# Cross attention's output projection as seven block products, its weight sums made on GpSimd and kept in DRAM

## The chip, the cores and the metric

The kernel runs on one core of one Trainium2 chip. The metric is the device time of one execution in microseconds (us). A core has five engines with a queue each: TensorE (PE in the profile, its weight loads PEld), VectorE (DVE), ScalarE (ACT), GpSimd (POOL) and SyncE (SP), which issues the DMAs. Each engine runs its own instructions in their order, and waits on semaphores for the others.

## The reference

One layer of an encoder on 1024 tokens of width 1024 in fp32: a mixer (window attention beside a gated delta rule), cross attention of 4 heads into 256 memory tokens, and a SwiGLU FFN, each with an RMSNorm before and after and a residual. The change is in the second of these, at `@ w_co`, and in what follows it up to the FFN's first products.

```python
def _memory_cross_attention(h, mem_n, w_q, w_kv, w_o):
    q = (h @ w_q).reshape(b, s, CROSS_HEADS, CROSS_HEAD_DIM)
    ...
    p = jax.nn.softmax(jnp.einsum('bqhd,bkhd->bhqk', q, k) * (CROSS_HEAD_DIM ** -0.5), axis=-1)
    o = jnp.einsum('bhqk,bkhd->bqhd', p, v).reshape(b, s, D_MODEL)
    return o @ w_o
...
c = _memory_cross_attention(_rms_norm(x, g_cross_pre), _rms_norm(mem, g_mem), w_cq, w_ckv, w_co)
x = x + _rms_norm(c, g_cross_post)
f = _swiglu(_rms_norm(x, g_ffn_pre), w_gate_up, w_down)
x = x + _rms_norm(f, g_ffn_post)
```

## The kernel before

Every matrix that goes into a product is split into a high part, rounded to the matmul's format by a cast on ACT, and a low part, the difference, on DVE or on POOL (`split`, L102 and L103). A product takes three matmuls: high by high, high by low, low by high. Weights come in pieces of 512 KB by `load_w` (L127): a DMA from SP into one of two buffers `wraw`, the cast to `whi`, the subtraction to `wlo`. A scheduler puts the instructions of each engine in an order before the kernel runs; `load_w` has a raised priority, so that pieces are asked for early, and the two buffers bound how early.

The tokens go in two halves of 512, four tiles of 128 each. **Cross attention** runs over 8 steps (half, head): `cross_q` makes two of the eight columns of q from two pieces of `w_cq`, whose low parts are POOL's; `cross_attention` is a generator that makes scores (`pcs`), softmax (`cpr`), transposes (`pct`) and the head's output (`pco`), and `go_on` lets it advance beside the steps that follow. Each output is split out of PSUM (`po`) into the place of q, in `q0` or `q1`, where it is the operand of the next product.

**The output projection** is `mid_gemm` with `w_co`, once for each half of the tokens and in it once for each half of the 1024 columns: four pieces of the weight by four token tiles by two row blocks by three matmuls, 96 matmuls of 512 columns, 384 in all (L1021). The last steps of the attention run inside the first of them (`rest`). Each result is squared on ACT for the norm (L1024) and multiplied by the gain on DVE (L1025). After both column halves the residual `xr` is loaded (L1031), the norm's factor comes from POOL (L1033, L1034), DVE makes the residual sum (L1035), which is stored, ACT squares it (L1038), POOL makes the next factor (L163, L164), and DVE scales it into `xr` (L1044).

**The turn.** `turned_k` transposes the normed tokens (L1187). For the first half that happens while the second half's projection runs: ACT scales `xraw` (L1192), casts it, and POOL subtracts the low part. For the second half it happens beside the FFN's first products (`pA0`, `EARLY` = 4 steps, L1224), whose results are copied to `m1` (L1241); the FFN itself works on block sums of the two halves (T1 to T4), made in that turn.

Of the kernel before, what the change touches and what calls it, by code (L numbers as in the profile page):

```python
# [19 lines left out]
P = 128  # L20
# [26 lines left out]
def host_constants():  # L47
# [24 lines left out]
    return out  # L72


@with_exitstack
def tile_hybrid_block(
# [112 lines left out]
    d_x1 = dram.tile([S, D], F32, name="d_x1")  # L189
    d_x2 = dram.tile([S, D], F32, name="d_x2")  # L190
# [780 lines left out]
    opB_first = [opB.tile([P, KT, HALF], t, tag=n, name=n) for n, t in ((b0, F32R), (b1, F32), (b2, F32R))]  # L971
# [3 lines left out]
    places = {"s1": ((opB, b0), (opB3, "b3")), "s2": ((opB, b1), (opB, b2))}  # L975

    def operand(pool_, tag):
        if tag in places:
            return [p_.tile([P, KT, HALF], F32R, tag=t, name=t) for p_, t in places[tag]]
        return [pool_.tile([P, KT, HALF], F32R, tag=f"{tag}{i}", name=f"{tag}{i}") for i in range(2)]  # L980
# [20 lines left out]
    def mid_gemm(tz, act, w, gp, res, dst, hf, between=None, eng=None, then=None, second=None):  # L1001
# [24 lines left out]
        xn = []  # L1026
        for t in range(4):
            tok = slice(hf * HALF + t * P, hf * HALF + (t + 1) * P)
            z = zs[t]
            xr = tz.tile([P, D], F32, tag="xr", name="xr", bufs=XR)  # L1030
            nc.sync.dma_start(xr, res[tok, :])  # L1031
            rs = tz.tile([P, 1], F32, tag="prs", name="prs", bufs=4)
            nc.gpsimd.tensor_scalar(rs, sss[t][:, 1:2], sss[t][:, 0:1], D * EPS, ALU.add, ALU.add)  # L1033
            nc.gpsimd.tensor_tensor(rs, rs, mhalf[:, 0:1], ALU.pow)  # L1034
            nc.vector.scalar_tensor_tensor(z, z, rs, xr, ALU.mult, ALU.add)  # L1035
            nc.sync.dma_start(dst[tok, :], z)
            s2 = tz.tile([P, 1], F32, tag="ps2", name="ps2", bufs=4)
            nc.scalar.activation(xr, z, AF.Square, accum_out=s2)  # L1038
            r2 = tz.tile([P, 1], F32, tag="pr2", name="pr2", bufs=4)
            rstd_of(r2, s2, 1.0 / D, EPS)  # L1040
            if hf and not eng:
                nc.scalar.activation(xr, z, AF.Identity, scale=r2)
            else:
                nc.vector.tensor_scalar(xr, z, r2, None, ALU.mult)  # L1044
            xn.append(xr)
        return xn
# [26 lines left out]
    h2T = [[opB.tile([P, KT, HALF], F32R, tag=b1, name=b1), opB_first[2]]]  # L1073
# [23 lines left out]
    def cross_attention(q, h):  # L1097
# [65 lines left out]
    def blocks(t):  # L1163
        return t[:, 0:HK], t[:, HK:KT]

# [387 lines left out]
```

## Time and profile before

| what | value |
|---|---|
| median of 3 runs | 1539.52 us (1538.82 to 1541.98) |
| the profiled execution | 1539.27 us |
| its span, in which the profile's times lie | 1537.3 us |
| granted TensorE clock | 0.99 |

The span is the time between the first and the last instruction that the profiler saw; the execution's time has 1.97 us around it. A row of the timeline begins with the start in the span and the length, then engine, line, operation, what is written and read, and in brackets how long the engine was idle before it and what ended that. A row such as "TENSOR_TENSOR wlo<-wraw,whi 128x1024" is one instruction on 128 partitions by 1024 elements; "x2" joins two in a row, with the length of both.

### The profile page before, as it was taken

Reading aid. Unit: us, or ns where it says so; the run is one execution under the profiler, and the core shown is the slowest. Engines: PE = TensorE matmul, PEld = TensorE weight load, DVE = VectorE, ACT = ScalarE, POOL = GpSimd, SP = SyncE. Lnnn points to the kernel's source line nnn. Section 1 sums busy time; section 2 is a strip of 40 time slices with the busy share of each in tenths; the row PEclk is TensorE's granted clock in tenths of the full one; section 3 lists DMA queues with packets and bytes.
Section 4 is the critical chain, followed back from the end, with each engine's and each line's share of the span. In section 5 each row is a group of like instructions: output and inputs, shape, how many; then the busy total and the mean of one; then the engine's idle time right before and its main releaser. Section 6 shows DMA issues by size and latency. Waiting matters only on the chain.

```text
span 1537.3 us, 20939 instructions
## 1 busy us (share of the span) xinstructions
PE 1485.0 (97%) x7451; PEld 1251.2 (81%) x7451; DVE 1062.2 (69%) x1762; ACT 713.2 (46%) x1377; POOL 307.0 (20%) x297
## 2 busy tenths in 40 slices
PE   6999999988999989999999999999999999999998
PEld 5888887877899878888888887888888888888786
DVE  6877898856989766445444487776877555696665
ACT  5665551336556765455444564323223332354532
POOL 2000110000004201252201432443433332000010
PEclk8999999999999999999999999999999999999999
DMA  6235456768997575354113554343533334852355
GB/s 207 76 112 142 121 154 153 223 170 257 326 312 249 167 272 177 116 192 137 55 56 99 185 195 130 120 133 110 172 123 96 110 103 158 287 189 95 107 177 166
DMA packets 267366, 247.16 MB, mean 161 GB/s; under 512 B 39016, under 2 KB 204797, under 8 KB 267261
## 3 DMA queue, kind: packets, MB, share of 16 engines
q1 hardware_dynamic: 267261, 245.82, 51.1%
q8 instruction: 59, 0.97, 0.3%
q14 instruction: 46, 0.38, 0.1%
HBM read 173.65 MB, written 69.50 MB: 158 GB/s over the span
## 4 chain that ended last, share of the span: by engine, by line
PE 82%; DVE 7%; DMA 3%; ACT 3%; issue 2%; SPq 1%; POOL 0%; DVEq 0%; POOLq 0%; ACTq 0%
PE pg L263 12%; PE pmg L1021 10%; PE pD L1224 8%; PE pE L1224 8%; PE pA L1224 8%; PE pcq L263 6%; PE pdX L1414 6%; PE pdA L1414 4%; PE pB L1224 4%; PE psc L787 2%; PE pdX L1507 2%; PE pdD L1414 2%; PE pcs L1108 1%; PE pco L1136 1%; PE pcv L934 1%
## 5 line engine op out<-in xcount | busy, mean ns | idle before, releaser
L102 ACT CAST whi<-wraw 128x1024 fp32r<-128x1024 f32 x108 | 113.4, 1050 | 174.9 <-PE pmg L1021 55.2
L103 DVE TENSOR_TENSOR wlo<-wraw,whi 128x1024 fp32r<-128x1024 f32 x78 | 95.2, 1221 | 85.6 <-ACT whi L102 78.6
L263 PE MATMUL pg<-hhi,whi 128*128 128x512 f32 x352 | 141.1, 402 | 1.5 <-DVE rop L732 1.3
L263 PE MATMUL pg<-hlo,whi 128*128 128x512 f32 x352 | 140.7, 400 | 0.0
L263 PE MATMUL pg<-hhi,wlo 128*128 128x512 f32 x352 | 140.3, 399 | 0.0
L1021 PE MATMUL pmg<-whi,b 128*128 128x512 f32 x384 | 116.1, 391 | 0.0
L1224 PE MATMUL pA<-s,whi 128*128 128x512 f32 x352 | 109.2, 391 | 1.0 <-ACT m L1241 1.0
L103 POOL TENSOR_TENSOR wlo<-wraw,whi 128x1024 fp32r<-128x1024 f32 x30 | 72.6, 2420 | 160.7 <-ACT whi L102 160.6
L1021 PEld LDWEIGHTS pmg<-whi,b 128*128 128x128 f32 x384 | 71.7, 188 | 14.5
L263 PEld LDWEIGHTS pg<-hhi,whi 128*128 128x128 f32 x352 | 67.3, 192 | 15.6 <-DVE rop L732 1.8
L263 PEld LDWEIGHTS pg<-hlo,whi 128*128 128x128 f32 x352 | 67.5, 192 | 13.3
L263 PEld LDWEIGHTS pg<-hhi,wlo 128*128 128x128 f32 x352 | 67.3, 191 | 13.2
L1414 PE MATMUL pdX<-dhl,whi 128*128 128x512 f32 x264 | 76.1, 390 | 1.5 <-DVE zv L1469 0.8
L1224 PEld LDWEIGHTS pA<-s,whi 128*128 128x128 f32 x352 | 65.5, 188 | 14.7 <-ACT m L1241 1.5
L1021 PE MATMUL pmg<-wlo,b 128*128 128x512 f32 x192 | 71.2, 390 | 0.0
L1224 PE MATMUL pA<-s,wlo 128*128 128x512 f32 x176 | 68.7, 391 | 0.0
L102 ACT CAST whi<-araw 128x1024 fp32r<-128x1024 f32 (+1 forms) x36 | 35.4, 982 | 71.3 <-PE pdX L1414 27.6
L1301 POOL TENSOR_TENSOR act<-act,up 128x512 f32<-128x512 f32 x33 | 50.2, 1520 | 89.4 <-DVE up L1300 53.1
L103 DVE TENSOR_TENSOR wlo<-araw,whi 128x1024 fp32r<-128x1024 f32 (+1 forms) x36 | 40.8, 1134 | 39.1 <-ACT whi L102 39.0
L288 DVE SCALAR_TENSOR_TENSOR acc<-cp,cols,acc 128x1024 f32<-128x1024 f32 x48 | 61.3, 1280 | 1.5 <-ACT acc L286 0.8
L1414 PEld LDWEIGHTS pdX<-dhl,whi 128*128 128x128 f32 x264 | 49.3, 188 | 12.8 <-issue 1.1
L102 ACT CAST dhl<-b 128x512 fp32r<-128x512 f32 x66 | 40.2, 619 | 32.8 <-PE pdA L1414 18.5
(410 smaller groups left out, 3950.9 us busy)
## 6 DMA issues: line engine op xcount, KB each, us to landing
wraw<-in_w_gate_up_dram SPq DMA_DIRECT2D x52, 512.0 KB, 4.0
kv<-d_kv SPq DMA_DIRECT2D x32, 512.0 KB, 6.7
wraw<-in_w_in_dram SPq DMA_DIRECT2D x22, 512.0 KB, 5.0
b<-in_w_down_dram SPq DMA_DIRECT2D x20, 512.0 KB, 6.9
araw<-d_as SPq DMA_DIRECT2D x20, 512.0 KB, 3.8
pz<-d_pz SPq DMA_DIRECT2D x32, 256.0 KB, 6.3
wraw<-in_w_ckv_dram SPq DMA_DIRECT2D x16, 512.0 KB, 7.1
wraw<-in_w_out_dram SPq DMA_DIRECT2D x16, 512.0 KB, 3.9
```

The source lines that it names most:

```text
L102: nc.scalar.copy(hi, src)
L103: (eng or nc.vector).tensor_tensor(lo, src, f32(hi), ALU.subtract)
L263: nc.tensor.matmul(p_, w[:, k, :], ah[a][:, k, :], start=(k == 0 and i == 0), stop=(k == nk - 1 and i == 2))
L288: nc.vector.scalar_tensor_tensor(acc, cp[:, t:t + S], taps[t], acc, ALU.mult, ALU.add)
L787: nc.tensor.matmul(out[:, d, h, :], lt[:, d, h, :], rt[:, d, h, :], start=True, stop=True)
L934: nc.tensor.matmul(pp[t], mT[a][:, k, t * P:(t + 1) * P], w[:, kk, :], start=(k == 0 and i == 0), stop=(k == KT - 1 and i == 2))
L1021: nc.tensor.matmul(pp[t], act[a][:, k, tt], w_[:, kk, :], start=(k == 0 and i == 0), stop=(k == KT - 1 and i == 2))
L1108: nc.tensor.matmul(pp[:, t2_, :], q[a][:, ct, tt], kr_[b_][:, ct, :], start=(j == 0 and i == 0), stop=(j == 1 and i == 2))
L1224: nc.tensor.matmul(out_, w[a][:, k, :], xx[b_][:, k, :], start=(start and k == 0 and i == 0), stop=(k == HK - 1 and i == 2), skip_group_ch ...
L1301: nc.gpsimd.tensor_tensor(o_, o_, up, ALU.mult)
L1414: nc.tensor.matmul(banks[t], a[:, k - k0, tt], w, start=(first and k == 0 and i == 0), stop=(k == NB - 1 and i == 2), skip_group_check=not ...
L1507: nc.tensor.matmul(X[t], a[:, k], w[:, k0 + k], start=False, stop=(k0 + k == NB - 1 and i == 2), skip_group_check=True)
```

## The change

The product of all tokens with `w_co` is written as a 2 by 2 block product (token halves by row halves, row halves by column halves) in Winograd's form, with seven products of blocks in the place of eight. Rows are regrouped so that block row r takes the 256-row pieces 2kp + r, which are the columns that the even or the odd heads made.

- The attention's outputs are copied to fp32 (`araw` for the first half, `araw1` for the second) before they are split. For the first half, and for the odd heads of the second, POOL makes the low part from the copy; before, it was DVE, out of PSUM.
- `weight_sums`: in steps 0, 1, 3 and 4 of the attention four blocks of `w_co` are loaded into the buffers of z, POOL makes four sums of them in place, 128 x 1024 each, and POOL issues their stores to `d_t` in DRAM, from which `load_w` fetches them later.
- `token_sums`: DVE makes four sums of token blocks and splits S1 and S2, for the first pair of heads inside the first product and for the second pair after it.
- The products, in order: q0's even heads by w11, then its odd heads by w21 on top, S2, S1 on top, S4 by w22, S3, and q1's odd heads on top; each is 48 matmuls.
- The first half's turn (`turn_first`) stands between the two halves of the last product; the residual's second four loads wait for it, since `xr` has four buffers.
- The second half's turn begins after one early step of the FFN instead of ahead of it, and T1's and T3's low parts go from DVE to POOL.

```diff
+    def attended(q, hf, h, j, po):
...
+        nc.scalar.copy(raw, po)
+        if h % 2 or not hf:
+            split(q[0][:, ct, :], q[1][:, ct, :], raw, eng=nc.gpsimd)
...
-            split(q[0][:, 2 * h + j, :], q[1][:, 2 * h + j, :], po)
+            attended(q, hf, h, j, po)
...
+    def weight_sums(step, kp):
+        if step == 0:
+            for t, rc in zip(wt, ((0, 0), (0, 1), (1, 1), (1, 0))):
+                nc.sync.dma_start(t, co(*rc, kp).rearrange("(k p) n -> p k n", p=P))
+        elif step == 1:
+            for o_, a, b_, d_ in ((b11, b12, b11, d_t[0]), (b12, b22, b12, d_t[1]), (b22, b22, b11, d_t[2]), (b21, b21, b22, d_t[3])):
+                nc.gpsimd.tensor_tensor(o_, a, b_, ALU.subtract)
+                nc.gpsimd.dma_start(d_[kp * 256:(kp + 1) * 256, :].rearrange("(k p) n -> p k n", p=P), o_)
...
-        turns.append(cross_attention(q, h))
...
+        turns.append(cross_attention(q, hf, h))
+        if i < 6:
+            weight_sums(i % 3, i // 3)
...
+    def token_sums(p):
+        k2 = slice(2 * p, 2 * p + 2)
+        a11, a12, a21, a22 = araw[2 * p], araw[2 * p + 1], araw1[2 * p], araw1[2 * p + 1]
+        nc.vector.tensor_tensor(a22, a21, a22, ALU.add)
+        nc.vector.tensor_tensor(a21, a11, a21, ALU.subtract)
+        nc.vector.tensor_tensor(a11, a22, a11, ALU.subtract)
+        split(S2h[:, k2], S2l[:, k2], a11)
+        nc.vector.tensor_tensor(a12, a12, a11, ALU.subtract)
+        split(S1h[:, k2], S1l[:, k2], a22)
...
-    xn = mid_gemm(tz, q0, w_co, gp, d_x1, d_x2, 0, then=rest)
+        if i == 1:
+            token_sums(0)
+
+    def token_product(banks, a, w, start=True, halves=False, then=None, between=None):
...
+            for t in ts:
+                for kk in range(2):
+                    k = 2 * kp + kk
+                    for i, (b_, c) in enumerate(((0, 0), (0, 1), (1, 0))):
+                        nc.tensor.matmul(banks[t], a[c](k, slice(t * P, (t + 1) * P)), pieces[kp][b_][:, kk, :],
...
+    token_product(A, heads(q0, 0), lambda kp: co(0, 0, kp), then=rest)
+    for t in range(4):
+        nc.scalar.copy(zz[t][:, HI], A[t])
+    token_product(A, heads(q0, 1), lambda kp: co(1, 0, kp), start=False, then=lambda kp: rest(2 + kp))
...
+    token_sums(1)
+    for t in range(4):
+        square(0, t, 0, A[t], zz[t][:, LO])
+        nc.vector.tensor_tensor(zz[t][:, LO], A[t], gp[:, LO], ALU.mult)
...
+    token_product(X, tiles((S2h, S2l)), summed(2))
+    for t in range(4):
+        nc.vector.tensor_tensor(z1[:, t, LO], zz[t][:, HI], X[t], ALU.add)
...
+        split(S4h[:, k2], S4l[:, k2], araw[2 * p + 1])
+    token_product(X, tiles((S1h, S1l)), summed(0), start=False)
...
+        split(S3h[:, k2], S3l[:, k2], araw1[2 * p], eng=nc.gpsimd)
+    X = four([(pg, "pg")] * 4)
+    token_product(X, tiles((S4h, S4l)), lambda kp: co(1, 1, kp), halves=True)
...
+        xn.append(normed(tz, 0, t, zz[t], zss[0][t], d_x1, d_x2))
+    X = four(others)
+    token_product(X, tiles((S3h, S3l)), summed(1))
+    for t in range(4):
+        z = z1[:, t, HI]
+        nc.vector.tensor_tensor(z, z, X[t], ALU.add)
+        square(1, t, 1, z)
+        scaled(z, HI, nc.gpsimd)
...
+    def turn_first():
+        for k in range(KT):
+            pt = turned_k(xn, k, (pg, "pg"))
+            nc.scalar.activation(raw[:, k, :], pt, AF.Identity, scale=gain("ffn", k))
+            split(x1h[:, k, :], x1l[:, k, :], raw[:, k, :], eng=nc.gpsimd)
...
+    token_product(X, heads(q1, 1), summed(3), start=False, halves=True, between=turn_first)
+    xn = []
+    for t in range(4):
+        z = z1[:, t, LO]
+        nc.vector.tensor_tensor(z, z, X[t], ALU.add)
+        square(1, t, 0, z)
+        scaled(z, LO)
+        xn.append(normed(tz, 1, t, z1[:, t], zss[1][t], d_x1, d_x2))
...
+            split(T1[0][:, k], T1[1][:, k], t1, eng=nc.gpsimd)
+            split(T3[0][:, k], T3[1][:, k], t3_, eng=nc.gpsimd)
...
+        if e == 1:
+            T1, T2, T3, T4 = turn_second()
```

Three places of the engines' orders follow. Numbers behind the names are buffers; with the change `split` is at L117 and L118.

On DVE, where the attention ends: before, the last head's two outputs are split and the wlo of the following pieces come.

```order
L1025 TENSOR_TENSOR z_7880<-pmg_7888,gpost_7875 128x512
L103 TENSOR_TENSOR wlo_8169<-wraw_8166,whi_8168 128x1024
L1025 TENSOR_TENSOR z_7881<-pmg_7889,gpost_7875 128x512
L103 TENSOR_TENSOR b2_7295<-pco_8124,b1_7294 128x512
L103 TENSOR_TENSOR b2_7295<-pco_8133,b1_7294 128x512
L103 TENSOR_TENSOR wlo_8199<-wraw_8196,whi_8198 128x1024
```

With the change, at the end of the attention and of the first pair of products (araw_6855, araw_6856, araw1_8056 and araw1_8163 are the outputs of heads 2 and 3 of the two halves; s00 and s01 are the high and low parts of S1 and S2, b0_8297 and b3_8298 those of S3 and S4):

```order
L1224 TENSOR_TENSOR araw1_8163<-araw1_8056,araw1_8163 128x1024
L1288 TENSOR_TENSOR z_6851<-pmg_7951,gpost_6846 128x512
L1225 TENSOR_TENSOR araw1_8056<-araw_6855,araw1_8056 128x1024
L118 TENSOR_TENSOR wlo_8266<-wraw_8263,whi_8265 128x1024
L1288 TENSOR_TENSOR z_6852<-pmg_7952,gpost_6846 128x512
L1226 TENSOR_TENSOR araw_6855<-araw1_8163,araw_6855 128x1024
L118 TENSOR_TENSOR b3_8298<-araw_6854,b0_8297 128x1024
L118 TENSOR_TENSOR s01_7940<-araw1_8163,s00_7939 128x1024
L1228 TENSOR_TENSOR araw_6856<-araw_6856,araw_6855 128x1024
L118 TENSOR_TENSOR s01_7940<-araw_6855,s00_7939 128x1024
```

The second s01 row is the low part of S2 that the S2 product's second half reads; nine instructions stand ahead of it from the first sum of these heads on.

On POOL, in the attention before, there is only the low part of each piece of `w_cq`:

```order
L103 TENSOR_TENSOR wlo_7299<-wraw_7296,whi_7298 128x1024
L103 TENSOR_TENSOR wlo_7392<-wraw_7389,whi_7391 128x1024
L103 TENSOR_TENSOR wlo_7443<-wraw_7440,whi_7442 128x1024
L103 TENSOR_TENSOR wlo_7536<-wraw_7533,whi_7535 128x1024
L103 TENSOR_TENSOR wlo_7587<-wraw_7584,whi_7586 128x1024
```

With the change the sums, their stores and the low parts of the heads' outputs stand between them:

```order
L1193 TENSOR_TENSOR z_6849<-z_6850,z_6849 128x1024
L118 TENSOR_TENSOR wlo_7352<-wraw_7349,whi_7351 128x1024
L1194 DMA d_t1_121<-z_6849 128x2x512
L1193 TENSOR_TENSOR z_6850<-z_6851,z_6850 128x1024
L1194 DMA d_t3_122<-z_6850 128x2x512
L1193 TENSOR_TENSOR z_6851<-z_6851,z_6849 128x1024
L118 TENSOR_TENSOR wlo_7445<-wraw_7442,whi_7444 128x1024
L1194 DMA d_t2_123<-z_6851 128x2x512
```

Three to four sums and stores now stand between one wlo and the next.

On ACT, in the turn of the first half: before, the groups come in pairs, with casts of weights and squares of the projection between them.

```order
L1192 ACTIVATE xraw_8328<-ptn_8331,cols_73 128x512
L1192 ACTIVATE xraw_8328<-ptn_8339,cols_73 128x512
L102 CAST s00_8329<-xraw_8328 128x512 x2
L102 CAST whi_8541<-wraw_8539 128x1024
L1192 ACTIVATE xraw_8328<-ptn_8347,cols_73 128x512
```

With the change, the last part of it, with the squares of the second half (z1) and the copies that free the early products' PSUM banks:

```order
L1345 ACTIVATE xraw_8228<-ptn_8677,cols_73 128x512
L117 CAST s00_8583<-xraw_8228 128x512
L1273 ACTIVATE jk_8761,zss_7948<-z1_8224 128x512
L117 CAST s00_8583<-xraw_8228 128x512
L1058 ACTIVATE xr_8713,ps2_8720<-z1_8224 128x1024
L117 CAST s00_8583<-xraw_8228 128x512 x2
L1058 ACTIVATE xr_8730,ps2_8737<-z1_8224 128x1024
L1058 ACTIVATE xr_8747,ps2_8754<-z1_8224 128x1024
L1407 COPY m1_8809<-pA0_8796 128x512
L1407 COPY m1_8831<-pA0_8818 128x512
```

Three wide squares (L1058), which need the residual sums of the second half, now stand ahead of the first m1 copy.

More of the change, by code (lines that the diff above doesn't have):

```diff
@@ L189, in tile_hybrid_block @@
     d_x1 = dram.tile([S, D], F32, name="d_x1")
+    d_t = [dram.tile([HALF, HALF], F32, name=f"d_t{n}") for n in (1, 3, 2, 4)]
     d_x2 = dram.tile([S, D], F32, name="d_x2")
@@ new lines, in summed, with four, heads, tiles @@
+    def summed(i):
+        return lambda kp: d_t[i][kp * 256:(kp + 1) * 256, :]
+    def four(pools):
+        return [p_.tile([P, 512], F32, tag=tag, name="pmg") for p_, tag in pools]
+    def heads(q, r):
+        return [lambda k, tt, t=t: t[:, 4 * (k // 2) + 2 * r + k % 2, tt] for t in q]
+    def tiles(t):
+        return [lambda k, tt, t_=t_: t_[:, k, tt] for t_ in t]
+    LO, HI = slice(0, HALF), slice(HALF, D)
+    zss = [[tz.tile([P, 2], F32, tag="zss", name="zss", bufs=8) for _ in range(4)] for _ in range(2)]
@@ L1214, in tile_hybrid_block @@
+    X22 = opC.tile([P, 2, HK, HALF], F32R, tag="x22", name="x22")
+    X22 = X22[:, 0], X22[:, 1]
     NF = FF // P
```

186 lines of the change are left out of this document (123 added, 63 removed).

## The prediction

> **What bounds the kernel now.** I read the shares of the engines first, then the chain that ended last, then the stretch that the change rewrites cut in four, then what TensorE (PE) waited for there.
>
> ```profile
> PE 1485.0 (97%) x7451; PEld 1251.2 (81%) x7451; DVE 1062.2 (69%) x1762; ACT 713.2 (46%) x1377; POOL 307.0 (20%) x297
> PE 82%; DVE 7%; DMA 3%; ACT 3%; issue 2%; SPq 1%; POOL 0%; DVEq 0%; POOLq 0%; ACTq 0%
> ```
>
> PE is busy 97% of the span and carries 82% of the chain: a matmul less is time less, unless PE then waits. The four stretches below are the end of the attention, the output projection of both halves, the start of the FFN, and its next 16 us. The columns are the stretch, PE, PEld, DVE, ACT and POOL busy, the granted clock (1.00 throughout), DMA share and GB/s.
>
> ```profile
> 786.40:821.00 34.60, 34.60 (x173) 29.31 (x172) 17.42 (x26) 15.10 (x31) 0.00 (x0) 1.00 0.20 61
> 821.00:890.00 69.00, 69.00 (x322) 57.38 (x321) 30.14 (x33) 34.36 (x62) 24.65 (x29) 1.00 0.46 153
> 890.00:937.00 47.00, 45.95 (x216) 37.19 (x215) 41.04 (x56) 31.91 (x54) 11.67 (x14) 1.00 0.54 180
> 937.00:953.00 16.00, 13.92 (x59) 10.58 (x58) 10.21 (x15) 3.96 (x8) 3.93 (x3) 1.00 0.48 149
> ```
>
> Until 890 PE never stops; all the others have room. From 890 to 953 it idles 1.05 + 2.08 = 3.1 us; the list of PE's waits has three there:
>
> ```profile
> PE pA L1224 <- ACT m L1241: 1.0, 1, 1.0
> PE pB L1224 <- DVE s1l L103: 1.0, 1, 1.0
> PE pD L1224 <- DVE u L1341: 1.0, 1, 1.0
> ```
>
> **What the change removes.** 8 x 48 = 384 matmuls of 512 columns become 7 x 48 = 336. The price of one is in the chain of waits (start, length, count):
>
> ```profile
> 821.17 31.96 PE pmg L1021 x141
> 922.97 0.87 PE ptn L1187 x8
> ```
>
> 31.96/141 = 0.2267 us, and a transpose 0.87/8 = 0.109. So 48 x 0.2267 = **10.9 us** go. Of the 3.1 us idle, the 1.05 at 893 is the wait for the m copy, which I price anew below, so it counts as gone; the other 2.08 come from late sums on DVE and POOL, and POOL now has four subtractions more of the same kind ahead of them, so I let them stand. Gain: 10.9 + 1.05 = **11.95** (bounds 10.9 and 10.9 + 3.1 = 14.0).
>
> **Place 1: the first token sums.** The S2 product's second pair of row blocks needs araw of the last head. The whole chain from that head's last matmul (pco) runs on ACT, POOL, DVE in the order shown with the change: copy out of PSUM, square, cast, low part on POOL, and then DVE's list down to the second "s01" row, because the sum overwrites araw and so waits for the cast and the low part. The prices are start-to-start times of neighbours that run back to back:
>
> ```profile
> 860.05 1.05 ACT L102 CAST whi<-wraw 128x1024 fp32r<-128x1024 f32 x1 [2.91 <-PE pmg L1021]
> 861.01 1.26 ACT L1192 ACTIVATE xraw<-ptn,cols 128x512 f32<-128x512 f32 x2
> 862.16 1.14 ACT L102 CAST s<-xraw 128x512 fp32r<-128x512 f32 x2
> 863.19 0.61 ACT L1024 ACTIVATE z<-pmg 128x512 f32<-128x512 f32 x1
> 863.87 0.60 ACT L1024 ACTIVATE z<-pmg 128x512 f32<-128x512 f32 x1
> 893.53 0.57 ACT L1241 COPY m<-pA 128x512 f32<-128x512 f32 x1
> 819.35 1.23 DVE L103 TENSOR_TENSOR wlo<-wraw,whi 128x1024 fp32r<-128x1024 f32 x1 [0.81 <-ACT whi L102]
> 820.49 0.68 DVE L1025 TENSOR_TENSOR z<-pmg,gpost 128x512 f32<-128x512 f32 x1
> 821.15 1.37 DVE L103 TENSOR_TENSOR b<-pco,b 128x512 fp32r<-128x512 f32 x2
> 856.70 2.55 POOL L103 TENSOR_TENSOR s<-xraw,s 128x512 fp32r<-128x512 f32 x2 [3.38 <-ACT s L102]
> ```
>
> ACT: wide cast 0.96, xraw 1.15/2 = 0.58, cast 1.03/2 = 0.515, square 0.68, copy 0.57. DVE: 1.14 for 1024 columns, 0.66 for a product out of PSUM. POOL: 2.55/2 = 1.27. The chain: 0.57 + 0.68 + 0.515 + 1.27 = 3.04, then eight DVE steps of 1024 columns, 9.12, and two z of 0.66, 1.32: 13.5 us. PE has 47 matmuls to run meanwhile (19 of the first product, 24 of S2's first pair, 4 that need only the high part): 47 x 0.2267 = 10.65. Left: **2.8 us** of waiting if nothing disturbs DVE.
>
> Something does. In POOL's order the two wide subtractions for S3 (b3 from araw1) fall due just when DVE walks this chain. Two engines that both read two SBUF operands disturb each other in this trace:
>
> ```profile
> 697.26 2.40 POOL L103 TENSOR_TENSOR wlo<-wraw,whi 128x1024 fp32r<-128x1024 f32 x1 [3.94 <-ACT whi L102]
> 703.81 2.40 POOL L103 TENSOR_TENSOR wlo<-wraw,whi 128x1024 fp32r<-128x1024 f32 x1 [4.15 <-ACT whi L102]
> 698.83 1.38 DVE L1118 TENSOR_TENSOR cpr<-cpr,csum 128x512 f32<-128x512 f32 x1
> 703.03 0.69 DVE L1118 TENSOR_TENSOR cpr<-cpr,csum 128x512 f32<-128x512 f32 x1
> 935.21 1.26 POOL L1273 TENSOR_TENSOR sr<-wraw 128x512 f32<-128x512 f32 x1 [34.48 <-DMA wraw<-in_w_gate_up_dram]
> 936.43 1.75 POOL L1275 TENSOR_TENSOR sr<-wraw 128x512 f32<-128x512 f32 x1
> 935.51 1.51 DVE L103 TENSOR_TENSOR b<-r,b 128x512 fp32r<-128x512 f32 x1
> 936.95 1.78 DVE L1274 TENSOR_TENSOR sr<-sr,wraw 128x512 f32<-128x512 f32 x1
> ```
>
> The same multiplication takes 0.69 alone and 1.38 when it starts inside POOL's 2.40; it ends at 700.2, 0.55 after POOL does. The pairs at 935 end one after the other, 936.47, 937.02, 938.18, 938.73. So they take turns: a wide POOL subtraction costs DVE up to its 2.40. Two of them are 4.8, less one z of 0.66, whose first operand is in PSUM and which can run beside POOL: 4.2. (Bounds 0, if they fall into DVE's waits, and 4.8.) **Place 1: 2.8 + 4.2 = 7.0.** [...]
>
> **Place 2: the turn of the first half inside the last product.** Before, the 32 transposes of the first half lie eight at a time among the second half's matmuls; now they stand between the halves of the last product, with few matmuls among them, and ACT must do all of what follows before it reaches the m1 copy that frees PE's bank (ACT's order is shown with the change): 8 xraw 4.64, 8 casts 4.12, 4 squares 2.72, one wide cast 0.96, 3 wide squares and the copy 0.57. A wide square:
>
> ```profile
> 891.45 1.05 ACT L1038 ACTIVATE xr<-z 128x1024 f32<-128x1024 f32 x1
> 892.49 1.05 ACT L1038 ACTIVATE xr<-z 128x1024 f32<-128x1024 f32 x1
> ```
>
> 3 x 1.04 = 3.12, and the sum is 16.1 us from the first transposed group. PE has 28 transposes, 3.05, and 32 matmuls, 7.25: 10.3. Wait: **5.8 us.** The wide squares also need the residual, whose four loads can start only when the last transposes have read the xr buffers, some 5 us after the first group:
>
> ```profile
> xr<-d_x SPq DMA_DIRECT2D x8, 512.0 KB, 9.3
> wraw<-in_w_co_dram SPq DMA_DIRECT2D x16, 512.0 KB, 3.8
> 841.80 2.48 DVE L1035 SCALAR_TENSOR_TENSOR z<-z,prs,xr 128x1024 f32<-128x1024 f32 x2
> ```
>
> The first lands between 3.8 (a load alone) and 9.3 (median of four together); the third residual sum (1.24 each) is then done at 5 + 8 + 1.24 = 14.2 for a third load that lands after 8, and copy and square behind it end at 15.9. So loads and ACT tie at 16; if all landed after 9.3 it would be 4 us more. POOL ties too: eight low parts of 1.27, 10.2, and some dozen small operations between them,
>
> ```profile
> 895.49 0.75 POOL L163 TENSOR_SCALAR pr<-ps 128x1 f32<-128x1 f32 x1
> 896.32 1.47 POOL L164 TENSOR_TENSOR pr<-pr,mhalf 128x1 f32<-128x1 f32 x1
> ```
>
> 4 to 6 us at these prices and somewhat less, from 2.35 after the first group: the last at 16.6 to 18.6, when PE asks for it at about 17.7. In that time DVE runs ten operations with two SBUF operands, 4 x 0.66 + 2 x 1.14 + 4 x 1.24 = 9.9 us. Taking turns costs POOL between 0 and 9.9; by the row at 936.43, 1.75 for 1.26, it is 0.49 for each of eight, 3.9, less about 1 of slack: **3.0** (0 to 9.9). Place 2: 5.8 + 3.0 = 8.8.
>
> **Costed at nothing.** *Weight sums*: eight subtractions of 2.40 on POOL, 19.2, and eight stores issued from POOL, in the attention, where the order alternates them with the wlo that PE needs. The wlo at 697.26 and 703.81 leave POOL 4.15 of each 6.55 us, and a sum is 2.40 beside a 1.27 low part now and then; a wlo may come some 4 us late, and load_w runs one piece (6.5 us) ahead. So 0; the upper bound is 4 us, if that cover is gone at one piece. No trace here shows a DMA issued from POOL; I take it within the same slack. [...] *Second half's turn*: from the m1 copy at 16.1, the fourth square, POOL's pair of 2.2, the scale and wlo end near 21.6, and PE comes to that weight at about 24: 0, and up to 4.5 if POOL and DVE alternate there too. *Loads of d_t and the seven products' own weights*: 14 pieces instead of 16, 0. *Residual adds out of PSUM* (12 of 0.66) lie beside products: 0.
>
> **Sum.** -11.95 + 7.0 + 8.8 = +3.85. On the profiled execution's 1539.27 that is **1543.1**; the median 1539.52 lies 0.25 above it, less than the 0.2% (3.1 us) that a measurement of this kernel can tell from no change.
>
> **Rivals.** *DVE and POOL hardly meet* (faster). If POOL's S3 pair runs before or behind DVE's chain at place 1, and its low parts fall between DVE's steps at place 2, the 4.2 and 3.0 are gone: 1539.27 - 11.95 + 2.8 + 5.8 = 1535.9. The point at which it decides is whether POOL's first b3 starts before DVE's first wide sum of that chain or after its last. For it: DVE's busy time in 821 to 890 is 30.14 of 69. Against it: the rows at 698 and 935. *The stalls are covered too*: the scheduler's prices put more matmuls ahead than I counted; with half of 8.6 waiting left, 1531.6. Against it: PE's order is fixed and is what I counted. *POOL starves the attention*: wlo late by 4 at both blocks of sums, so 8 more: 1551. For it: POOL's order there puts two wide sums around each wlo; against it: 4.15 idle before each now.
>
> **How the numbers follow.** Forecast 0.46 (1539 to 1548), hardly meet 0.26 (1533 to 1539), covered 0.10, starved 0.18. The range 1532 to 1552 leaves out most of the covered case and half of the starved one, 0.17; it takes in the loads at +4. Faster by over 0.2% (under 1536.2): 0.14 of the second case and 0.10 of the third, 0.24. Within: 0.12 of the second and 0.16 of the forecast, 0.28. Slower (over 1542.4): 0.30 + 0.18 = 0.48.
>
> **What would show it.** PE should wait about 7 us for s01 in the S2 product, with DVE's subtractions there at up to 3.5 instead of 1.2; some 9 us around the turn and the first pA0, for xraw, for POOL's s01 and for the m1 copy; nothing in the attention, with POOL's wlo within one piece. If the waits at s01 are under 4, the turns were priced wrong; if PE waits at pcq for wlo, the weight sums do it; if the residual loads name the wait at place 2, the buffers do.

## The result, and the profile after

| what | before | after |
|---|---|---|
| median time | 1539.17 us (4 runs, 1537.78 to 1541.98) | 1559.63 us (4 runs, 1556.46 to 1560.79) |
| the profiled execution, its span | 1539.27 us, 1537.3 | 1556.46 us, 1554.8 |
| granted TensorE clock | 0.99 | 0.983 |

The changed kernel takes 1.0127 times as long, with an interval of 1.0106 to 1.0149: 20 us more by the medians, 17.5 us by the spans of the two profiles. It is slower, as forecast, but far above the 1543.1 and the range that ended at 1552. The profile pictured is the fastest of the four runs of after; the 3 us to the median are not in it.

The first two lines of the profile after, busy times and the chain that ended last:

```profile
PE 1485.0 (96%) x7403; PEld 1247.2 (80%) x7403; DVE 1100.7 (71%) x1766; ACT 727.5 (47%) x1399; POOL 374.1 (24%) x339
PE 77%; DVE 8%; DMA 4%; ACT 3%; issue 2%; POOL 2%; SPq 1%; DVEq 0%; POOLq 0%; ACTq 0%
```

Here lies the first oddity: 48 matmuls fewer (the records show 7403 for 7451), and PE is busy for the same 1485.0 us. The matmuls that are left are listed with more time. The stretches show where. The first three lines are before, the next three after: from the attention's first `pcq` to the first `pmg` of the projection, from there to the first `pA`, and on to the first `pD`. The columns are those of the prediction.

```profile
656.50:786.40 129.90, 129.90 (x694) 111.74 (x692) 62.34 (x108) 63.99 (x132) 42.82 (x26) 1.00 0.36 114
786.40:889.94 103.54, 103.54 (x494) 86.63 (x492) 47.49 (x58) 49.41 (x92) 24.59 (x29) 1.00 0.37 122
889.94:943.59 53.65, 51.52 (x237) 41.16 (x236) 47.60 (x64) 34.41 (x58) 12.91 (x14) 1.00 0.49 164
```

```profile
658.94:791.92 132.98, 130.80 (x694) 111.67 (x693) 73.97 (x98) 68.14 (x140) 77.59 (x50) 1.00 0.50 160
791.92:897.81 105.89, 95.36 (x445) 78.56 (x444) 73.54 (x80) 55.08 (x97) 35.68 (x33) 0.97 0.34 112
897.81:960.28 62.47, 56.79 (x236) 43.35 (x237) 49.85 (x56) 38.88 (x67) 34.82 (x28) 0.92 0.52 176
```

Read length and PE's busy time against each other:

| stretch | longer by | PE busy | PE idle |
|---|---|---|---|
| ahead of the first `pcq` | 2.4 | +2.3 | +0.1 |
| attention | 3.1 | +0.9 | +2.2 |
| projection and turn | 2.35 | -8.2 | +10.5 |
| early FFN | 8.8 | +5.3 | +3.55 |
| the rest | 0.8 | -0.3 | +1.1 |
| sum | 17.5 | 0.0 | +17.5 |

In the projection 48 matmuls of 0.2267 us, 10.9, are gone, but PE's busy time falls only by 8.2: 2.7 came back. In the early FFN the same 236 or 237 instructions are busy 5.3 us longer. Both stretches have a granted clock under 1.00, as neither had before. In the first one the chain's piece "840.53 23.78 PE pmg L1252 x96" makes it plain: 96 matmuls at 0.2267 would be 21.8. Slices of 1 us each, behind the wait for `xraw` at 897.81 (the granted clock is the third column from the end):

```profile
898.00:899.00 1.00, 1.00 (x5) 0.77 (x5) 0.80 (x1) 1.00 (x4) 1.00 (x1) 0.88 1.03 414
899.00:900.00 1.00, 1.00 (x4) 0.57 (x3) 0.98 (x1) 1.00 (x3) 1.00 (x2) 0.50 0.90 348
900.00:901.00 1.00, 1.00 (x3) 0.84 (x3) 1.00 (x2) 1.00 (x4) 1.00 (x1) 0.50 0.98 393
901.00:902.00 1.00, 1.00 (x4) 0.78 (x3) 1.00 (x3) 1.00 (x4) 0.92 (x2) 0.50 0.95 377
902.00:903.00 1.00, 1.00 (x6) 0.83 (x5) 0.82 (x1) 1.00 (x2) 1.00 (x1) 0.91 0.83 273
```

PE runs without a gap there, at half clock, for 0.24 + 3 + 0.18 = 3.4 us, and then at full clock again. Two other pieces are twice as long, one from inside the wait for S2's low part on, one in the early FFN:

```profile
837.32:844.15 6.83, 3.62 (x9) 2.85 (x10) 6.11 (x6) 1.04 (x1) 0.00 (x0) 0.50 0.35 112
909.00:915.83 6.83, 5.03 (x12) 3.36 (x12) 2.43 (x3) 2.69 (x4) 6.41 (x9) 0.50 0.40 154
```

What PE waited for from 620 to 980 (sum, times, longest):

```profile
PE pmg L1252 <- DVE s L118: 6.1, 1, 6.1
PE pA L1368 <- POOL s L118: 2.4, 3, 1.8
PE pco L1168 <- ACT cpr L1147: 2.1, 2, 1.1
...
PE pA L1368 <- ACT xraw L1345: 1.9, 1, 1.9
PE pA L1368 <- ACT m L1407: 1.5, 1, 1.5
PE pmg L1252 <- DVE z L1336: 1.5, 1, 1.5
...
PE pmg L1252 <- ACT s L117: 1.0, 1, 1.0
```

6.1 and 1.0 are place 1 of the prediction; POOL's s, xraw and m are place 2; `pco` and `z` it did not name. Place 1 looks as it was drawn, DVE first, POOL behind it:

```profile
831.52 3.40 DVE L118 TENSOR_TENSOR b<-araw,b 128x1024 fp32r<-128x1024 f32 x1
834.85 3.35 DVE L118 TENSOR_TENSOR s<-araw,s 128x1024 fp32r<-128x1024 f32 x1
```

```profile
830.42 6.70 POOL L118 TENSOR_TENSOR b<-araw,b 128x1024 fp32r<-128x1024 f32 x2 [4.85 <-ACT b L117]
```

Two DVE subtractions that take 1.2 elsewhere take 3.4 while POOL makes its two wide ones. In the attention it is not the wide ones that suffer. DVE's scaling of the softmax's maximum, two numbers for each partition, and what POOL did meanwhile:

```profile
736.54 5.52 DVE L1143 TENSOR_SCALAR cmx<-cmx 128x2 f32<-128x2 f32 x1
```

```profile
736.39 2.54 POOL L118 TENSOR_TENSOR b<-araw,b 128x512 fp32r<-128x512 f32 x2
738.87 0.72 POOL L1194 DMA_DIRECT2D d_t<-z  x1
739.62 2.41 POOL L1193 TENSOR_TENSOR z<-z 128x1024 f32<-128x1024 f32 x1
```

The small operation ends at 742.06, as the last of the three subtractions of POOL does (742.03). It did not get in between them. `cpr` on ACT waits for it, and PE for `cpr`, 1.00 us at 743.23.

### The profile page after: what moved, and what is told of

Its sections match the earlier page's. It is cut to its first block, busy times and chain, and to the rows that moved or that the text cites. A ratio compares the mean times of both kernels' runs of the same rounds, so it can differ in the third digit from the quotient of the medians.

```text
span 1554.8 us, 20969 instructions
## 1 busy us (share of the span) xinstructions
PE 1485.0 (96%) x7403; PEld 1247.2 (80%) x7403; DVE 1100.7 (71%) x1766; ACT 727.5 (47%) x1399; POOL 374.1 (24%) x339
## 4 chain that ended last, share of the span: by engine, by line
PE 77%; DVE 8%; DMA 4%; ACT 3%; issue 2%; POOL 2%; SPq 1%; DVEq 0%; POOLq 0%; ACTq 0%
PE pg L279 13%; PE pE L1368 8%; PE pD L1368 7%; PE pA L1368 6%; PE pdX L1580 6%; PE pcq L279 5%; PE pmg L1041 4%; PE pdA L1580 4%; PE pB L1368 4%; PE pmg L1252 3%; PE psc L803 2%; PE pdX L1673 2%; PE pdD L1580 2%; PE pcs L1140 1%; PE pco L1168 1%
## 5 line engine op out<-in xcount | busy, mean ns | idle before, releaser
L117 ACT CAST whi<-wraw 128x1024 fp32r<-128x1024 f32 x106 | 111.3, 1050 | 173.1 <-PE pmg L1252 29.1
L118 DVE TENSOR_TENSOR wlo<-wraw,whi 128x1024 fp32r<-128x1024 f32 x76 | 95.3, 1253 | 67.4 <-ACT whi L117 62.2
L1368 PE MATMUL pA<-s,whi 128*128 128x512 f32 x352 | 112.8, 401 | 5.8 <-POOL s L118 2.4
L118 POOL TENSOR_TENSOR wlo<-wraw,whi 128x1024 fp32r<-128x1024 f32 x30 | 72.7, 2424 | 120.0 <-ACT whi L117 119.9
L117 ACT CAST whi<-araw 128x1024 fp32r<-128x1024 f32 (+1 forms) x36 | 35.3, 982 | 71.2 <-PE pdX L1580 24.4
L118 DVE TENSOR_TENSOR wlo<-araw,whi 128x1024 fp32r<-128x1024 f32 (+1 forms) x36 | 40.8, 1132 | 38.2 <-ACT whi L117 38.0
L1440 DVE TENSOR_TENSOR sr<-sr,wraw 128x512 f32<-128x512 f32 x22 | 37.1, 1688 | 36.4 <-POOL sr L1439 36.4
L117 ACT CAST s0h<-sr 128x512 fp32r<-128x512 f32 x22 | 13.7, 623 | 94.6 <-POOL sr L1439 94.6
L1368 PE MATMUL pB<-b,s1h 128*128 128x512 f32 x176 | 54.6, 391 | 2.8 <-ACT s1h L117 2.1
L1611 POOL TENSOR_TENSOR frs<-frs,mhalf 128x1 f32<-128x1 f32 x8 | 8.1, 1020 | 204.2 <-DVE frs L1610 204.2
```

What stands on the lines that cost most here:

```text
L117: nc.scalar.copy(hi, src)
L118: (eng or nc.vector).tensor_tensor(lo, src, f32(hi), ALU.subtract)
L1368: nc.tensor.matmul(out_, w[a][:, k, :], xx[b_][:, k, :], start=(start and k == 0 and i == 0), stop=(k == HK - 1 and i == 2), skip_group_ch ...
L1440: nc.vector.tensor_tensor(s[1], s[0], a_[:, 0:HK], ALU.subtract)
```

## The experiments

All are the changed kernel with one edit (the last three with several), in one run each beside a run of the kernel before on the same chip (1544.03 for the fillers at place 1, S3 on DVE, the sums left out and the scaling on ACT; 1543.77 for the sums on DVE, the cover, the early turn and the filled turn; 1541.27 for the relieved turn and the first two that put edits together); the last has its own comparison. These three times of one kernel lie 2.8 us apart, more than some of the edits bring, so stretches of the profiles are compared, not times.

### Half clock at place 1: filler matmuls

```diff
...
+            if fill and n == 1:
+                keep = pg.tile([P, 512], F32, tag="pg", name="keep")
+                for _ in range(fill):
+                    tc.keep_in_program_order(nc.tensor.matmul(keep, a[0](0, slice(0, P)), pieces[0][0][:, 0, :], start=True, stop=True))
...
-    token_product(X, tiles((S2h, S2l)), summed(2))
+    token_product(X, tiles((S2h, S2l)), summed(2), fill=28)
```

> 28 matmuls that compute nothing needed are put on TensorE where it waits 6.15 us for S2's low part. Theory (the clock falls because TensorE stands still): the wait shrinks to about 0 to 1 us at the same end, the granted clock stays 1.00 after it, and the 96 matmuls of S2's second half and S1 that take 23.78 us in the changed kernel take 96 x 0.2267 = 21.8. Rival (the matmuls there are slow for what they read or for other engines' traffic): they still take about 23.8 us.

Measured: 1554.28 us. The wait falls from 6.15 to 1.15, the clock stays at 1.00, and the stretch from the S2 product to the first transposes falls from 63.79 to 62.13, by 1.66:

```profile
839.27 0.50 PE L1256 MATMUL pmg<-whi,s 128*128 128x512 f32 x1 [1.15 <-DVE s L118]
```

Work that nobody needs makes this stretch shorter: with 28 matmuls where PE waited, its clock is 1.00 for the change's 0.95. The half clock here is a cost of the wait in its own right.

### Taking turns at place 1: S3's low parts on DVE

```diff
-        split(S3h[:, k2], S3l[:, k2], araw1[2 * p], eng=nc.gpsimd)
+        split(S3h[:, k2], S3l[:, k2], araw1[2 * p])
```

> The two wide low parts for S3 go from POOL to DVE, so that POOL does nothing while DVE makes the sums. Theory (the two engines take turns): the two DVE subtractions that took 3.40 and 3.35 us take 1.2 each, DVE has two more of 1.14, and the wait for S2's low part falls from 7.1 us (0.97 + 6.15) to about 4.9. Rival (these two are slow by themselves, or for DMA traffic): they stay at 3.4 and the wait grows to about 9.4.

Measured: 1558.38 us. Waits of 0.97 and 4.09, 5.06 in all for 7.12:

```profile
834.70 1.20 PE L1252 MATMUL pmg<-whi,s 128*128 128x512 f32 x4 [0.97 <-ACT s L117]
839.99 0.80 PE L1252 MATMUL pmg<-whi,s 128*128 128x512 f32 x1 [4.09 <-DVE s L118]
```

DVE has two subtractions more, 2.4 us at the 1.21 of the change, and PE waits 2.06 less. POOL's two instructions had cost DVE more than that: 3.40 + 3.35 for 2 x 1.21, 4.3.

### The attention: sums left out, moved, and one operation moved

Three edits: the subtractions left out, their engine changed, and the scaling of the maximum taken from DVE.

```diff
-                nc.gpsimd.tensor_tensor(o_, a, b_, ALU.subtract)
```

> The eight weight subtractions on POOL are left out; blocks of w_co itself are stored in their place, so the four products by sums compute something else; loads and stores stay. Theory (POOL's back-to-back wide operations keep DVE's small cmx scaling waiting, 2.2, 3.6, 5.5 and 3.8 us instead of 0.16): these fall to about 0.2 and the attention, from the first matmul of q to the first of the projection, goes from 132.97 us to about 130. Rival (the stores issued from POOL or the four extra loads cost it): 133 stays.

```diff
-                nc.gpsimd.tensor_tensor(o_, a, b_, ALU.subtract)
+                nc.vector.tensor_tensor(o_, a, b_, ALU.subtract)
```

> The eight weight subtractions go from POOL to DVE; POOL still issues the stores. Attention from the first matmul of q to the first of the projection: 132.98 us in the changed kernel, 129.90 in the kernel before. Theory (POOL's long runs of wide operations keep DVE out): about 130 to 131, cmx at 0.16 nearly everywhere, DVE 9 us more. Rival (any engine with 9 to 19 us more work there is late): 133 or more.

```diff
-            nc.vector.tensor_scalar(mxs[:, 2 * tp:2 * tp + 2], mxs[:, 2 * tp:2 * tp + 2], -1.0 / 16.0, None, ALU.mult)
+            nc.scalar.mul(mxs[:, 2 * tp:2 * tp + 2], mxs[:, 2 * tp:2 * tp + 2], -1.0 / 16.0)
```

> The scaling of cmx by -1/16 goes from DVE to ACT; POOL's sums and stores stay. Theory (that one small DVE operation is what gets stuck behind POOL): the attention goes from 132.97 us to about 130.5, though the other DVE operations with two operands still take up to 2.4 us more here and there. Rival (POOL's own low parts of w_cq come late): TensorE still loses 3 us, waiting for wlo or for pcq's operands.

Measured: without the subtractions 1558.46 us, the attention 130.89 long (132.98 with them, 129.90 before), one wait of 0.75 left. So 2.1 of the 3.1 us are theirs; the loads, the stores, the copies and POOL's other new work have at most the 1.0 that is left. The scaling takes there what it takes alone, 0.15 to 0.18, but for one of 1.65 and one of 0.33 among the ten between 700 and 755:

```profile
736.95 0.17 DVE L1143 TENSOR_SCALAR cmx<-cmx 128x2 f32<-128x2 f32 x1
```

With the sums on DVE: 1560.57 us, the attention 136.42. Half the price for most of them (1.21 instead of 2.40), and still worse, as the rival said: DVE stands in the way of its own softmax, PE waits 2.92 for `cpr`, and the granted clock of the stretch falls to 0.97. With the scaling on ACT: 1556.88 us, but the attention takes 133.37. The theory that this one operation was the cause fell. The next one that DVE has in the chain met the same fate:

```profile
724.27 7.00 DVE L1150 TENSOR_TENSOR cpr<-cpr,csum 128x512 f32<-128x512 f32 x1
```

POOL is busy beside it without a pause, as beside the scaling of 5.52 in the change. So what delays DVE in these two runs is POOL's work beside it, whichever of the two operations meets it (5.52 for 0.17, 7.00 for 0.69). That it is the unbroken run and not the work as such, no run here shows by itself.

### Cover for place 1 from useful work

S4 does not need the last head's sums. Its product's first half is put ahead of the S2 product's second half, where the fillers stood. `part` issues one of the two halves of a `token_product`, `split4(p)` makes the low part of S4 for pair p.

```diff
-    token_product(X, tiles((S2h, S2l)), summed(2))
...
+    split4(0)
+    X = four(others)
+    part(X, tiles((S2h, S2l)), load_w(summed(2)(0), 2, 512), 0)
+    Y = four([(pg, "pg")] * 4)
+    part(Y, tiles((S4h, S4l)), load_w(co(1, 1, 0), 2, 512), 0)
+    part(X, tiles((S2h, S2l)), load_w(summed(2)(1), 2, 512), 1)
...
```

> The first half of the S4 product (24 matmuls, 5.4 us), which needs nothing of the last head, is put ahead of S2's second half. From the first S2 matmul to the first transpose of the turn the changed kernel takes 63.79 us. Theory (TensorE stands still 7.1 us for a chain on DVE and POOL, and pays some 2 us of half clock for standing still): 63.79 - 5.4 - 1.7 = 56.7, and less where POOL's S3 work no longer meets the chain; no granted clock under 1.00 there. Rival (the chain gets longer by S4's low part, which now stands ahead, or the clock falls anyway): 59 to 61.

Measured: 1551.07 us. The stretch falls from 63.79 to 56.90, as the theory had it. The change first, then this run:

```profile
826.61:890.40 63.79, 55.17 (x234) 44.48 (x232) 48.20 (x49) 26.91 (x44) 25.29 (x22) 0.95 0.39 131
826.04:882.94 56.90, 53.56 (x234) 43.19 (x233) 47.88 (x49) 26.79 (x44) 25.38 (x22) 1.00 0.43 147
```

The clock stays at 1.00, and the same 234 instructions are busy 1.6 us less. The wait for S2's low part is gone; one of 1.86 for S4's low part and the one of 1.47 for `z` remain.

### The turn: earlier, filled, relieved

The turn written ahead of the last product:

```diff
-    token_product(X, heads(q1, 1), summed(3), start=False, halves=True, between=turn_first)
+    turn_first()
+    token_product(X, heads(q1, 1), summed(3), start=False, halves=True)
```

> The turn of the first half is written ahead of the last product instead of between its halves, so that some 27 more of that product's matmuls (6 us) lie behind most of it. Stage: from the first S2 matmul to the first pD of the FFN, 133.67 us in the changed kernel (S2's own first wait included). Theory (place 2 lacks cover: ACT and POOL have 16 to 18 us of work behind 10 us of matmuls): about 128 to 129, the waits for xraw, POOL's s and the m1 copy mostly gone, about 1 us of wait new ahead of the first transposes. Rival (the second half's own residual chain sets the end): not under 132.

Measured: 1558.02 us; from the S2 product to the first `pD` 136.3 us for 133.7. The theory fell, and the rival's "not under 132" held. The copy of `m` is waited for longer (4.13 for 1.52), and the second half's `xr`, not a wait before, adds 1.58 and 0.76: what moved is the place of the wait, since the second half's norm still has to come after the last product.

Twenty filler matmuls ahead of the first `pA`:

```diff
+            if e == 0 and i == 0:
+                for _ in range(20):
+                    tc.keep_in_program_order(nc.tensor.matmul(A[0], X11[0][:, 0, 0:P], X11[0][:, 0, :], start=True, stop=True))
```

> 20 matmuls that compute nothing needed (4.5 us at full clock) stand ahead of the first pA0 product. From the first pA0 matmul to the first pD the changed kernel takes 62.47 us. Theory (some 5 us of waits and some 4 us of half clock are in it, both for lack of work on TensorE): the 20 more cost nothing, 59 to 62.5 with them included, clock 1.00 from the fill on. Rival (the waits there stand behind TensorE's own products): 66 to 67.

Measured: 1556.81 us, 63.61 from the first `pA` to the first `pD`, fillers included, 1.14 more than without. 20 x 0.2267 = 4.5 us went in and 3.4 of them were absorbed. PE idles 4.25 us in this stretch (the change: 5.68), so 1.4 are waits that closed up; it is busy 59.36 (56.79), 2.6 more and not 4.5, so 2.0 are busy time that was not lost, with a clock of 0.95 for 0.92. Neither number that had been set down was hit, and the clock was not 1.00 from the fill on.

All of the turn's work of POOL on DVE:

```diff
-        scaled(z, HI, nc.gpsimd)
+        scaled(z, HI)
...
-            split(x1h[:, k, :], x1l[:, k, :], raw[:, k, :], eng=nc.gpsimd)
+            split(x1h[:, k, :], x1l[:, k, :], raw[:, k, :])
...
-            split(T1[0][:, k], T1[1][:, k], t1, eng=nc.gpsimd)
-            split(T3[0][:, k], T3[1][:, k], t3_, eng=nc.gpsimd)
+            split(T1[0][:, k], T1[1][:, k], t1)
+            split(T3[0][:, k], T3[1][:, k], t3_)
```

> All that the change gave to POOL in the two turns goes to DVE: the eight low parts of the first half's turn, the four products by the gain, T1's and T3's low parts; POOL keeps the small operations of the norms. From the first pA0 to the first pD the changed kernel takes 62.47 us, the kernel before 53.65. Theory (POOL's queue is what holds place 2: its wide low parts stand ahead of the norm factors that the second half's residual sums wait for, and block DVE): the waits for POOL go, the m copy's too, no half clock after them, 56 to 58. Rival (ACT's 16 us set it, or DVE becomes late with 10 us more): 61 or more.

Measured: 1551.55 us, the stretch 60.20 for 62.47. POOL's waits are gone, but the wait for the copy of `m` grew to 3.40, and the clock is 0.94. So POOL is a part of place 2 and ACT's order another, between theory and rival.

### Put together

Cover and relief in one kernel, then the low parts of the heads' outputs on DVE too, then the weight sums in pairs behind POOL's own last item with the second block one step later:

> The early half of the S4 product (as before) and the move from POOL to DVE in the turns together. Theory: both gains add, from the first S2 matmul to the first transpose about 57, from the first pA0 to the first pD 56 to 58; against the changed kernel some 12 us less, 1544 to 1546 for a profile like the first one. Rival: DVE is now the late one and the second gain is under 2 us.

```diff
-            split(q[0][:, ct, :], q[1][:, ct, :], raw, eng=nc.gpsimd)
+            split(q[0][:, ct, :], q[1][:, ct, :], po)
```

> As the last, and the low parts of the heads' outputs too go back to DVE, out of PSUM, in the attention; POOL has there the weight sums and stores alone besides its wlo. Attention from the first matmul of q to the first of the projection: 132.98 us in the changed kernel. Theory (DVE is kept out by POOL's unbroken runs, which get shorter): 131 to 132; the chain of the last head loses POOL's 1.27 and the copy's wait, so the wait ahead of S2's second half is gone. Rival (each sum by itself delays the softmax): 133.

```diff
...
-        elif step == 1:
+        else:
-            for o_, a, b_, d_ in ((b11, b12, b11, d_t[0]), (b12, b22, b12, d_t[1]), (b22, b22, b11, d_t[2]), (b21, b21, b22, d_t[3])):
-                nc.gpsimd.tensor_tensor(o_, a, b_, ALU.subtract)
+            for o_, a, b_, d_ in ((b11, b12, b11, d_t[0]), (b12, b22, b12, d_t[1]), (b22, b22, b11, d_t[2]), (b21, b21, b22, d_t[3]))[2 * step - 2:2 * step]:
+                with tc.issue_after(pooled[-1].ins):
+                    nc.gpsimd.tensor_tensor(o_, a, b_, ALU.subtract)
...
-        if i < 6:
-            weight_sums(i % 3, i // 3)
+        if i < 3 or 3 < i < 7:
+            weight_sums(i % 4 if i > 3 else i, i // 4)
...
+            with tc.high_priority(AHEAD):
+                nc.scalar.copy(a1, A[i])
```

> The last version with its three remaining waits taken up one by one: the weight sums are issued in pairs behind GpSimd's own last item of a group instead of back to back (the wide operations no longer run unbroken beside VectorE), those of the second block begin one step later, and the copies of the turn's second A are put ahead of wider work on ScalarE. Theory (what is lost in the attention is GpSimd's unbroken run, and what is left in the turn is an order on ScalarE): the attention, from its first output product to the projection, goes from 134.9 to 130-132 us, the wait for the copy of m from 3.4 to under 1.5, the time to 1535-1540 us, so 0 to 0.4% below the kernel before. Rival (what GpSimd does in the attention costs VectorE the same wherever it stands, and the turn is bound by the second half's own chain): attention 134 or more, first pA to first pD 57 or more, the time 1541-1545.

Measured: 1547.55 us, then 1542.08 us, where the kernel before took 1541.27. In the first the two stretches are 58.13 and 58.19, each a little over what had been hoped for. In the second the waits for S2's operand are gone as expected, but the attention rose to 134.92: a weight sum held up the low part of a piece that PE needed, 2.96 us, the case that the prediction had called starving. The paced one has a median of 1544.17 us (12 runs, 1538.23 to 1550.58) for 1541.74 (17 runs), a ratio of 1.0022 with an interval of 1.0007 to 1.0036. It is 2.4 us over the kernel before on its chip, where the change was 20 over: some 18 us better than the change, but no better than the kernel before. The 1535 to 1540 that was hoped for was missed. Its three stretches:

```profile
658.97:789.34 130.37, 130.29 (x694) 111.73 (x692) 72.75 (x106) 67.48 (x140) 67.90 (x42) 1.00 0.50 163
789.34:889.80 100.46, 93.60 (x445) 77.44 (x443) 76.14 (x90) 55.26 (x97) 20.67 (x22) 1.00 0.36 119
889.80:948.02 58.22, 52.18 (x237) 41.23 (x237) 50.95 (x70) 38.05 (x67) 14.14 (x14) 1.00 0.54 182
```

The attention is within 0.5 us of before, as expected. The clock is 1.00, and the same 236 or 237 instructions of the last stretch that were busy 56.79 in the change are busy 52.18. But PE still idles 6.86 us in the second stretch (before: none) and 6.04 in the third (before: 2.13), 10.8 us more in all, and the 48 matmuls were worth 10.9. The 6.86 are four waits: 1.35 and 2.15 at place 1, which are back, 1.47 for `z` and 1.90 for `xraw`. The last of them, and the longest of the third stretch:

```profile
889.80 0.72 PE L1387 MATMUL pA<-s,whi 128*128 128x512 f32 x2 [1.90 <-ACT xraw L1364]
...
897.90 0.73 PE L1387 MATMUL pA<-s,whi 128*128 128x512 f32 x2 [2.35 <-ACT m L1427]
```

ACT comes to the copy of `m` without a pause, and the higher priority did nothing for it: eight `xraw`, eight casts, the squares of the second half and two wide squares stand ahead, the same as in the version before it, where the wait was 2.37.

## Why the prediction was wrong

**The gain** (10.9 and 1.05). The 10.9 is right: about 48 records are gone from the projection's stretch. The 1.05 was read at the wrong place. The copy of `m` at 893.53 kept nobody waiting before; the wait in the list belongs to a later copy:

```profile
936.36 0.73 PE L1224 MATMUL pA<-s,whi 128*128 128x512 f32 x2 [1.03 <-ACT m L1241]
```

In the change no wait for `m` stands there and a new one, 1.52, stands at an earlier copy, so the term came out, but by luck.

**Place 1** (2.8 + 4.2 = 7.0). Right, 0.97 + 6.15 = 7.1, by the mechanism named: the subtractions at 3.40 and 3.35 had been given as "up to 3.5", and the run with S3's low parts on DVE came to 5.06 for an expected 4.9. The rival that DVE and POOL hardly meet fell at its own deciding point: POOL's first wide subtraction starts at 830.42, between DVE's first sum of the chain (825.60) and its last low part (839.26). That a `z` out of PSUM runs beside POOL at its own price, as the 0.66 taken off there has it, stands in the profile before: two take 1.37 at 863.92, inside two low parts of POOL that take 2.54 from 862.85.

**Place 2** (5.8 + 3.0 = 8.8). Right in what is waited for (`xraw`, `m`, POOL's s), too high in size: idle time grew by 1.9 ahead of the first `pA` and 3.55 behind it, 5.45, and with the wait of 1.05 that was counted as gone it is 6.5, 2.3 under the 8.8. The three waits that it named add up to less, 1.9 + 1.5 + 2.4 = 5.8. Beside it stands a wait of 1.5 for `z`, the residual add out of PSUM that was to "lie beside products: 0". In all, the two places were to bring 7.0 + 8.8 - 1.05 = 14.75 us of idle time, and PE idles 10.5 + 3.55 = 14.1 more.

**The step that failed** is the one that turned idle time into time. The prediction read 1.00 in the column of the granted clock and let every matmul cost 0.2267 behind a wait as well. Behind the new waits PE's busy time is 2.7 us over the price of its matmuls in the projection and 5.3 in the early FFN, **8.0 us**, nearly half of what separates the profiles, and no term stood for it. Without it the profiled time would be 1556.46 - 8.0 = 1548.5, inside the range.

Some 6 of the 8.0 are the half clock: PE is busy 3.62 + 3.41 + 5.03 = 12.06 us in the three pieces shown above, and half of that is 6.0; against runs with a clock of 1.00 it is 1.6 (the cover) and 4.6 (the paced version, 56.79 for 52.18), 6.2. The filler run shows the cause by itself: with the wait cut to 1.15 there is no half clock behind it, and the stretch is 1.66 us shorter in spite of 28 matmuls more. The rest, nearly 2 us, stands behind waits at full clock too: the paced version is busy 93.60 where 103.54 - 10.9 = 92.6 is the price, and 52.18 for 51.52. The first matmul behind a wait is listed with 0.50 us (the filler run's row), one without a wait with 0.39; that this is all of the rest is not shown.

The half clock has a length of its own: in the slices of eleven runs (the change and ten of the edits) it starts and ends on a grid of 3.413 us, whose place differs from run to run. With that goes another observation: the wait of 1.90 for `xraw` is the same in twelve of the kernels profiled here, and half clock follows it within 4 us in five of them (the change among them) and in the other seven not. The grid tells them apart as far as it is seen: in the five the whole wait lies between two of its edges (to 0.03 us), in five of the seven an edge cuts 0.05 to 0.66 us off it, and the other two, the last two versions put together, show no half clock in their slices that would place it. The piece of the grid that holds most of the wait, in the change and in the version with cover and relief:

```profile
895.35:898.76 3.41, 1.51 (x10) 1.14 (x9) 2.40 (x2) 3.41 (x7) 3.33 (x4) 1.00 0.56 207
892.11:895.52 3.41, 1.90 (x8) 1.59 (x9) 2.27 (x4) 3.41 (x8) 0.86 (x2) 1.00 0.90 314
```

PE is busy 1.50 to 1.54 us of this piece in the five and 1.55 to 1.90 in the five others. In none of them does PE stand still for the whole 3.41: a wait of 1.90 us was followed by half clock in five runs, and where it fell on the grid sets them apart. No sharp limit follows from so few pieces, and what makes the grid is not shown here.

**Costed at nothing: weight sums.** Failed too: the attention is 3.1 us longer, inside the bound of 4 that had been given, but for another reason. The prediction asked whether POOL would be late with `wlo`, and it was not (no `pcq` waits in the list). It did not ask whom POOL would keep waiting: DVE's chain of the softmax. It had counted only DVE's operations with two operands in SBUF as exposed; the 128x2 scaling has one. It took 5.52 us for 0.17 all the same, held through three instructions of POOL and the issue of a store. Without the subtractions 2.1 of the 3.1 us are gone; pacing them, with the heads' low parts off POOL, gave back 2.6.

**What the prediction could have no term for.** The 2.4 us ahead of the first `pcq` lie before the first instruction that was edited, 2.3 of them PE's busy time on the same matmuls; over all profiles here that point lies between 656.3 and 660.3, in kernels with the same code up to it. The 0.8 behind the first `pD` were not traced to a cause. Together they are 3.2 of the 17.5 us.

The sum by the same steps is then 3.85 - 0.65 (idle time overestimated) + 8.0 + 3.1 + 3.2 = 17.5, the difference of the spans. The likeliest case had the two waits right; the range was too narrow, because it combined the places' prices but held no row for what a place costs afterwards.

Left open: how place 2 divides between ACT's order and the second half's own chain. With POOL's work taken off and the cover put in, some 58 instead of 53.65 us remained, in three versions within 0.5 us of each other, and nothing that was tried went lower than 57.77.

## What to carry to other kernels

Price a new wait on a full TensorE at its length and then ask what follows: where the profile shows a clock of 1.00 with no waits, it has not shown what a wait costs, and here the aftermath was 8 us beside 14 of waiting, some 6 of them half clock. Matmuls that have to be done anyway, put ahead of the waiting ones, can be worth more than the time they fill: 24 of them, 5.4 us, took 6.9 us off. Matmuls that nobody needs gained 1.66 us at the one place and lost 1.14 at the other. Work for an idle GpSimd is not free because GpSimd is idle (here its eight sums made the attention 2.1 us longer): count the small VectorE operations in the chain beside it. Gaps between its wide instructions were tried only together with other edits; with them the attention came back to within 0.5 us.

## What was not expected of the hardware

- Half clock in pieces of 3.4 us or a multiple of it, after waits as short as 1.9 us; after the same wait of 1.90 in five runs of twelve and not in the others, by where it falls on a grid of 3.413 us, as far as the slices show that.
- A VectorE operation of 0.17 us that took 5.52, through three instructions of GpSimd and a DMA issue between them; VectorE did not get in there where one GpSimd instruction ended and the next began.
- The reverse also occurs: with the turn's low parts on DVE, a GpSimd operation on one number for each partition, 0.30 in the kernel before (840.36), took 4.57 while DVE was busy without a pause (in the version with the heads' low parts on DVE too):

```profile
893.01 4.57 POOL L1053 TENSOR_SCALAR prs<-zss 128x1 f32<-128x1 f32 x1 [2.44 <-ACT jk L1273]
```

- Issuing a store of 512 KB from GpSimd occupied it for 0.72 to 0.94 us, eight times in the change.
